# Merge of the DeltaNet inverse in 64x64 quadrants, five unnormalised projections at the start of layer 1, and sums of squares finished on VectorE

## The chip, the cores and the metric

The kernel runs on one core of a Trainium2 chip. The metric is the device time of one execution in microseconds (us), lower is better.

## The reference, cut to what matters

One inference step of a two-layer backbone: 128 context tokens and 256 latent tokens of width 1024, everything in float32. In each layer a modulated RMSNorm feeds one input projection, that feeds three token mixers (windowed attention, multi-head latent attention called MLA below, and a bidirectional gated DeltaNet); a gated sum of the three is projected back and added to the tokens; a second modulated norm and a squared-ReLU MLP follow.

```python
mod = silu(cond) @ w_ada + b_ada                          # shifts, scales and gates of both norms
y = mixer(rmsnorm(x, norm1_g) * (1 + sc1) + sh1)          # w_in, three mixers, w_branch, gates, w_out
x = x + g1 * y
h = rmsnorm(x, norm2_g) * (1 + sc2) + sh2
x = x + g2 * (square(relu(h @ w_ff1)) @ w_ff2)
# DeltaNet, for every chunk of 64 tokens, head and direction:
a_mat = where(strict, (kb @ kc.T) * decay, 0)             # 64 x 64, strictly triangular
t_mat = triangular_solve(eye + a_mat, eye)                # its inverse is wanted
u = t_mat @ (vc * beta);  w = t_mat @ (kb * exp(gc))
```

## The kernel before, in words

All activations lie transposed in SBUF, features on the 128 partitions and the 384 tokens along the row, so a projection is 128x128 weight blocks times 128x384 activations. Each weight tile is split on the chip into a rounded part `whi` (a cast on ScalarE, L147) and the rest `wlo` (a subtraction on VectorE, L148), and a product is three matmuls of 128x384 (`mm3`, L150 to L153: wh·rh, wh·rl, wl·rh; the right side is split in the same way, as `hh` and `hl` for the normed tokens). All other products are plain float32 matmuls through `mm` (L156); one such call shows as two PE instructions in the trace, a bf16 matmul and a transpose as one.

Work is put into three streams with priorities: "chain" (the mixers, whose steps wait for one another), "fill" (projections that are always ready) and "last". A scheduler lays out each engine's order when the kernel is built; on the chip every engine runs its own instructions strictly in that order. So TensorE's fill `mm3` stand between the steps of a chain, in a fixed number. PSUM has eight banks: three "g" (pool `pg`, projections), one "o", two "c" (`bank()`, all small chain products) and a pair "f" (`twin()`).

**Sums of squares and row broadcasts.** `squares` (L207) squares the token tiles on ScalarE and adds them on VectorE (L215), all but the last one, which goes apart. `sums` sums both parts over the partitions with matmuls against a column of ones (six `mm` a call, 128x1). `rsqrt` takes the inverse root on small VectorE operations; `rows` spreads a column over all partitions: `pieces` (L182 to L185) cuts it into three bf16 parts and three bf16 matmuls a row add them. `rstd_rows` is sums, rsqrt and rows in one.

**Start of layer 1 (L461 to L490).** The tokens are the output of layer 0's MLP. While the norm's inverse roots are worked out, two projections (`w_small`, whose output becomes the tile `kab`, and the DeltaNet column 11 of `w_in`) run on tokens that are scaled (`scaled`) but not normalised; then `modulated` (VectorE L227 and L230, ScalarE L229) makes the normalised `hh` and `hl` of all eight token tiles, and the two outputs are multiplied by the inverse roots afterwards (L482 to L487).

**Merge of the inverse (L857 to L899, tiles `Xi`).** Per chunk pair n (3) and direction d (2), four heads at once: M holds the 128x128 matrices. The diagonal 32x32 blocks are inverted on VectorE (L840 to L853, tiles `blk`), transposed as Xc and XcT, and spread into block-diagonal X0 and X0T (L870). Then 32-blocks are joined to 64 and 64 to 128 with five products p1 to p5: p1 and p3 of 128x128, p2 with 64 columns, p4 and p5 of 64x64, each with a PSUM read behind it on VectorE or ScalarE (L878, L886, L888, L895, L897). `M5` (L865) is M times a mask, `M2` (L867) a copy of a corner. GpSimd copies some of M's blocks (L828) and clears the tile of the inverse (L842).

**Modulation.** `ada` multiplies `silu(cond)` by `w_ada` in the fill stream of layer 0's branch merges (`merge(2, more, ...)`, `merge(1, more, ...)`), `ada_sums` does the same for later rounds on VectorE, a step per turn, within ff1 (the MLP's first product) and ff2.

Of the kernel before, what the change touches and what calls it, by code (L numbers as in the profile page):

```python
# [18 lines left out]
P = 128  # L19
DM = 1024  # L20
KT = DM // P
# [23 lines left out]
def trunk(ctx: ExitStack, tc: tile.TileContext, A, O):  # L45
# [57 lines left out]
    mask5 = [cst[:, C_M5 + d * P:C_M5 + (d + 1) * P] for d in range(2)]  # L103
# [3 lines left out]
    bdmask = cst[:, C_BD:C_BD + P]  # L107
# [80 lines left out]
    def rows(b, j0, n):  # L188
# [7 lines left out]
    def sums(ps, col, parts, n):  # L196
        for j in range(n):
            for i, sq in enumerate(parts):
                mm(ps[:, col + j:col + j + 1], sq[:, j * P:(j + 1) * P], ones1, i == 0, i == len(parts) - 1)

    def rstd_rows(parts, scale):

        ps = bank()
        sums(ps, 0, parts, 3)
        return rows(pieces(rsqrt(ps[:, 0:3], 3, scale)), 0, 3)
# [71 lines left out]
    def ada(l, rounds):  # L277

        for r in rounds:
            ps = bank(pg, "g")  # L280
            for k in range(KT):
                for half in range(2):
                    c0 = r * 2048 + half * 1024
                    raw = mk(ada_pool[0], [P, 1024], ada_pool[1], bufs=ada_pool[2])
                    nc.sync.dma_start(raw, A["w_ada"][l, k * P:(k + 1) * P, c0:c0 + 1024])
                    rv = raw.rearrange("p (b g i) -> p g b i", b=8, g=4)
                    for g in range(4):
                        mm(ps[32 * g:32 * g + 32, half * 256:half * 256 + 256].rearrange("p (b i) -> p b i", b=8),
                           cs[:, k, :], rv[:, g], start=k + half == 0, stop=k + half == KT)
                    if k + half == KT:  # L290
                        modulation(l, r, ps)
                    yield

    def ada_sums(l, rounds, pool):


        pick = mk(pool, [P, 2, 32], "pick")
        V.memset(pick, 0.0)
        for s in range(2):
            V.memset(pick[:, s, s:s + 1], 1.0)  # L300
        for r in rounds:
            ps = bank(pg, "g")
            for q in range(4):
                acc = mk(pool, [P, 2, 512], "aacc", bufs=1)
                c0 = r * 2048 + q * 512
                for k in range(KT):
                    raw = mk(pool, [P, 512], "araw", bufs=3)
                    nc.sync.dma_start(raw, A["w_ada"][l, k * P:(k + 1) * P, c0:c0 + 512])
                    for s in range(2):
                        if k == 0:  # L310
                            S.activation(acc[:, s, :], raw, AF.Copy, scale=cs[:, k, s:s + 1])
                        else:
                            V.scalar_tensor_tensor(out=acc[:, s, :], in0=raw, scalar=cs[:, k, s:s + 1], in1=acc[:, s, :],  # L313
                                                   op0=ALU.mult, op1=ALU.add)
                    if k == KT - 1:
                        for s in range(2):
                            av = acc[:, s, :].rearrange("p (b g i) -> p g b i", b=4, g=4)
                            for g in range(4):
                                mm(ps[32 * g:32 * g + 32, q * 128:q * 128 + 128].rearrange("p (b i) -> p b i", b=4),
                                   pick[:, s, :], av[:, g], start=q + s == 0, stop=q + s == 4)  # L320
                        if q == 3:
                            modulation(l, r, ps)
                    yield
# [134 lines left out]
    for l in range(DEPTH):  # L458
# [5 lines left out]
        else:  # L464
# [6 lines left out]
            for w in weights([A["w_small"][l], A["w_in"][l, 11]]):  # L471
                wh, wl = (t.rearrange("p (k c) -> p k c", k=KT) for t in w)
                M = wh.shape[2]
                ps = mk(pg, [P, 512], "g")[:M, :T + 2]
# [4 lines left out]
            for i, ps in enumerate(pss):  # L479
                M = ps.shape[0]  # L480
                t = mk(sp, [48, T], "kab", bufs=1) if i == 0 else mk(sp, [P, T], "sqacc", bufs=1)
                b = mk(sp, [P, 2], "eb")[:M]  # L482
                V.tensor_copy(b, ps[:, T:])
                S.copy(t, ps[:, :T])
                V.tensor_tensor(out=t, in0=t, in1=rb[:M], op=ALU.mult)
                for s, c in STREAMS:
                    S.activation(t[:, c], t[:, c], AF.Identity, bias=b[:, s:s + 1], scale=1.0)  # L487
                early.append(t)
# [50 lines left out]
        kab = early.pop(0)  # L539
        if l == 0:  # L540
            ps, kab = kab, mk(sp, [48, T], "kab", bufs=1)
            S.copy(kab, ps)
        nc.sync.dma_start(O["krT"][l], kab[0:32, 0:128])
        if l == 0:
            nc.sync.dma_start(cst[:, C_M5:], A["const"][:, C_M5:])
            tri = mk(sp, [P, T], "tmp")[:, :2 * P]
# [12 lines left out]
        def g4():  # L559
            return mk(ccp, [P, 4, P], "g", bufs=24)  # L560
# [4 lines left out]
        def h4():  # L565
            return mk(ccp, [P, 4, 64], "h", bufs=3)
# [164 lines left out]
        keys, queries = (mk(ccp, [P, 4, T], "kq", bufs=2) for _ in range(2))  # L731
        done = [conv_silu(ps, 4 + i, keys[:, i, :]) for i, ps in enumerate(early)]
# [56 lines left out]
        for n in range(3):  # L789
# [28 lines left out]
            for d in range(2):  # L818
# [5 lines left out]
                for b in range(4):  # L824
# [31 lines left out]

        Xi = {}  # L857
        half = (slice(0, 64), slice(64, 128))
        for n in range(3):
            for d in range(2):  # L860
                u0 = (2 * n + d) * 4
                hs, os = half[d], half[1 - d]
                M = Mg[n, d]
                M5 = g4()
                V.tensor_tensor(out=M5, in0=M, in1=mask5[d].unsqueeze(1).to_broadcast([P, 4, P]), op=ALU.mult)  # L865
                M2 = h4()
                V.tensor_copy(M2[hs], M[hs, :, os])  # L867
                X0, X0T = M, g4()
                for dst, c in ((X0T, (Xc, XcT)[d]), (X0, (XcT, Xc)[d])):
                    V.tensor_tensor(out=dst.rearrange("p h (b c) -> p h b c", b=4),  # L870
                                    in0=c[:, u0:u0 + 4, :].unsqueeze(2).to_broadcast([P, 4, 4, 32]),
                                    in1=bdmask.rearrange("p (b c) -> p b c", b=4).unsqueeze(1).to_broadcast([P, 4, 4, 32]),
                                    op=ALU.mult)
                ps = bank()
                for h in range(4):
                    mm(ps[:, h * P:(h + 1) * P], M5[:, h, :], X0T[:, h, :])
                WT = g4()
                S.copy(flat(WT), ps)  # L878
                pt = bank()
                for h in range(4):  # L880
                    mm(pt[hs, h * 64:h * 64 + 64], X0[:, h, hs], WT[:, h, hs])
                ps = bank()
                for h in range(4):
                    mm(ps[:, h * P:(h + 1) * P], WT[:, h, :], X0[:, h, :])
                X1T = h4()
                V.tensor_tensor(out=X1T[hs], in0=X0T[hs, :, hs], in1=pt[hs, 0:256].rearrange("p (h c) -> p h c", h=4),  # L886
                                op=ALU.subtract)
                V.tensor_tensor(out=flat(X0), in0=flat(X0), in1=ps, op=ALU.subtract)  # L888
                ps = bank()
                for h in range(4):  # L890
                    mm(ps[os, h * 64:h * 64 + 64], M2[hs, h, :], X1T[hs, h, :])
                W2 = h4()
                S.copy(W2[os].rearrange("p h c -> p (h c)"), ps[os, 0:256])
                ps = bank()
                for h in range(4):  # L895
                    mm(ps[hs, h * 64:h * 64 + 64], W2[os, h, :], X0[os, h, os])
                V.tensor_scalar(out=X0[hs, :, os], in0=ps[hs, 0:256].rearrange("p (h c) -> p h c", h=4), scalar1=-1.0,  # L897
                                scalar2=None, op0=ALU.mult)
                Xi[n, d] = X0  # L899
# [83 lines left out]
        r = pieces(r)  # L983
# [134 lines left out]
        for t in range(NF):  # L1118
# [12 lines left out]
            next(more, None)  # L1131
# [15 lines left out]
    sums(ps, 0, squares(x), 3)  # L1147
# [132 lines left out]
```

## Time and profile before

| what | value |
|---|---|
| median of 3 runs | 1564.96 us (1561.77 to 1565.35) |
| the profiled execution | 1564.52 us |
| its span, first to last instruction | 1562.7 us |
| PE busy | 1521.6 us (97%) |
| DVE, ACT, POOL busy | 1013.9 us (65%), 771.8 us (49%), 12.9 us (1%) |

PE is the matrix engine (TensorE), DVE VectorE, ACT ScalarE, POOL GpSimd. A busy PE is one that has a matmul under way; it says nothing about how much of its array that matmul fills. The 1.8 us between the profiled time and the span lie before the first and after the last instruction.

### The profile page before, as it was taken

What the parts mean: (1) busy time and instruction counts of PE and PEld (TensorE: products, weight loads), DVE (VectorE), ACT (ScalarE), POOL (GpSimd) and SP (SyncE); (2) the same over time, 40 slices, a digit from 0 to 9 for tenths busy, and PEclk for the clock granted to TensorE, in tenths of its full rate; (3) what the DMA queues carried; (4) which work ended last, traced back from release to release, by engine and by line L of the source; (5) the groups of instructions that cost most, each with busy time, mean ns of one, the idle gap of its engine ahead of it and who ended that gap; (6) DMA issues with size and microseconds to landing.
All of it is one profiled execution on the core that took longest, in us unless ns stands there. A gap on an engine that the chain in (4) does not pass through costs nothing.

```text
span 1562.7 us, 25131 instructions
## 1 busy us (share of the span) xinstructions
PE 1521.6 (97%) x9652; PEld 1396.2 (89%) x9652; DVE 1013.9 (65%) x2187; ACT 771.8 (49%) x1522; POOL 12.9 (1%) x34
## 2 busy tenths in 40 slices
PE   5999999999999999999999999999999999999998
PEld 3898788987888999999988987889888999999997
DVE  4667896475435877789986778955655565553332
ACT  3466633346524666643344676334465446664222
POOL 0000100000000000000000001000000000000000
PEclk9999999999999999999998999999999999999999
DMA  9532131143488555578763331311424434433332
GB/s 315 162 103 88 48 95 48 59 145 105 141 291 279 160 175 176 176 236 259 252 187 98 95 95 47 96 49 58 129 61 135 130 118 126 126 122 129 128 122 81
DMA packets 80857, 212.82 MB, mean 136 GB/s; under 512 B 8801, under 2 KB 24545, under 8 KB 80609
## 3 DMA queue, kind: packets, MB, share of 16 engines
q1 hardware_dynamic: 80736, 211.21, 42.7%
q8 instruction: 76, 1.25, 0.3%
q14 instruction: 45, 0.36, 0.1%
HBM read 204.59 MB, written 4.75 MB: 134 GB/s over the span
## 4 chain that ended last, share of the span: by engine, by line
PE 86%; DVE 8%; DMA 4%; ACT 1%; issue 1%; SPq 0%; DVEq 0%; ACTq 0%
PE g L151 22%; PE g L153 22%; PE g L152 22%; PE c L156 9%; PE f L156 3%; DMA araw<-in_w_ada_dram 2%; PE o L156 2%; PE f L443 2%; DVE wlo L148 2%; PE g L156 1%; DVE h L847 1%; DVE blk L849 1%; DMA mraw<-in_w_ada_dram 1%; PE c L151 1%; PE c L153 1%
## 5 line engine op out<-in xcount | busy, mean ns | idle before, releaser
L147 ACT CAST whi<-raw 128x1024 fp32r<-128x1024 f32 x268 | 280.8, 1048 | 463.6 <-PE g L152 408.0
L153 PE MATMUL g<-hh,wlo 128*128 128x384 f32 (+1 forms) x1440 | 495.2, 345 | 2.8 <-DVE wlo L148 2.7
L151 PE MATMUL g<-hh,whi 128*128 128x384 f32 (+1 forms) x1440 | 494.8, 345 | 3.1 <-ACT hh L229 1.5
L152 PE MATMUL g<-hl,whi 128*128 128x384 f32 (+1 forms) x1440 | 493.6, 344 | 1.3 <-DVE hl L230 1.0
L148 DVE TENSOR_TENSOR wlo<-raw,whi 128x1024 fp32r<-128x1024 f32 x268 | 326.0, 1217 | 168.5 <-PE g L153 123.1
L151 PEld LDWEIGHTS g<-hh,whi 128*128 128x128 f32 x1440 | 272.2, 189 | 14.9 <-issue 6.3
L153 PEld LDWEIGHTS g<-hh,wlo 128*128 128x128 f32 x1440 | 272.5, 189 | 12.4 <-DVE wlo L148 6.0
L152 PEld LDWEIGHTS g<-hl,whi 128*128 128x128 f32 x1440 | 272.2, 189 | 8.1 <-issue 2.7
L151 PE MATMUL g<-fh,whi 128*128 128x384 f32 x512 | 172.9, 338 | 0.0
L152 PE MATMUL g<-fl,whi 128*128 128x384 f32 x512 | 172.1, 336 | 0.0
L153 PE MATMUL g<-fh,wlo 128*128 128x384 f32 x512 | 172.1, 336 | 0.0
L313 DVE SCALAR_TENSOR_TENSOR aacc<-araw,cs,aacc 128x512 f32<-128x512 f32 x168 | 116.5, 747 | 11.0 <-DMA araw<-in_w_ada_dram 6.9
L151 PEld LDWEIGHTS g<-fh,whi 128*128 128x128 f32 x512 | 96.2, 188 | 1.6 <-issue 1.6
L152 PEld LDWEIGHTS g<-fl,whi 128*128 128x128 f32 x512 | 96.3, 188 | 0.0
L153 PEld LDWEIGHTS g<-fh,wlo 128*128 128x128 f32 x512 | 96.3, 188 | 0.0
L156 PE MATMUL c<-g,g 128*128 128x128 f32 (+1 forms) x608 | 77.5, 274 | 3.6 <-DVE g L870 3.1
L156 PEld LDWEIGHTS c<-g,g 128*128 128x128 f32 (+1 forms) x608 | 69.9, 182 | 11.3 <-ACT g L878 4.0
L151 PE MATMUL g<-brh,whi 128*128 128x384 f32 x192 | 66.4, 346 | 0.4 <-ACT whi L147 0.4
L152 PE MATMUL g<-brl,whi 128*128 128x384 f32 x192 | 65.7, 342 | 0.0
L153 PE MATMUL g<-brh,wlo 128*128 128x384 f32 x192 | 65.6, 342 | 0.0
L424 ACT ACTIVATE at_p<-at_p,at_nm 128x384 f32<-128x384 f32 (+1 forms) x96 | 51.8, 541 | 24.7 <-DVE at_nm L421 23.9
L148 DVE TENSOR_TENSOR fl<-fa,fh 128x384 fp32r<-128x384 f32 x64 | 35.6, 556 | 41.9 <-ACT fh L147 41.9
(312 smaller groups left out, 1862.3 us busy)
## 6 DMA issues: line engine op xcount, KB each, us to landing
raw<-in_w_ff_dram SPq DMA_DIRECT2D x128, 512.0 KB, 3.6
raw<-in_w_in_dram SPq DMA_DIRECT2D x102, 512.0 KB, 3.6
araw<-in_w_ada_dram SPq DMA_DIRECT2D x96, 256.0 KB, 3.4
raw<-in_w_branch_dram SPq DMA_DIRECT2D x24, 512.0 KB, 3.6
araw<-in_w_ada_dram SPq DMA_DIRECT2D x24, 512.0 KB, 6.4
raw<-in_w_out_dram SPq DMA_DIRECT2D x16, 512.0 KB, 4.3
mraw<-in_w_ada_dram SPq DMA_DIRECT2D x8, 512.0 KB, 9.2
mraw<-in_w_ada_dram SPq DMA_DIRECT2D x16, 256.0 KB, 7.6
```

The costliest lines, as they stand in the source:

```text
L147: S.copy(hi, src)
L148: V.tensor_tensor(out=lo, in0=src, in1=hi.bitcast(F32), op=ALU.subtract)
L151: PE.matmul(ps, lhsT=wh, rhs=rh, start=start, stop=False)
L152: PE.matmul(ps, lhsT=wh, rhs=rl, start=False, stop=False)
L153: PE.matmul(ps, lhsT=wl, rhs=rh, start=False, stop=stop)
L156: return PE.matmul(ps, lhsT=lhsT, rhs=rhs, start=start, stop=stop)
L313: V.scalar_tensor_tensor(out=acc[:, s, :], in0=raw, scalar=cs[:, k, s:s + 1], in1=acc[:, s, :], op0=ALU.mult, op1=ALU.add)
L424: S.activation(sm[:, :nk], sm[:, :nk], AF.Exp, bias=nm[:, u:u + 1], scale=-1.0, accum_out=den[:, u:u + 1])
L443: PE.transpose(pt[:, j * P:(j + 1) * P], ps_[half, n][:, c * P:(c + 1) * P], ident)
L847: V.tensor_tensor(out=tmp, in0=Cb[:, j + 1:, j:j + 1].to_broadcast([P, r, w]), in1=X[:, j:j + 1, :w].to_broadcast([P, r, w]), op=ALU.mult)
L849: V.tensor_tensor(out=X[:, j + 1:, :w], in0=X[:, j + 1:, :w], in1=tmp, op=ALU.subtract)
```

## The change: what it does

1. `sums` and `squares`: all squares are added on VectorE, one addition more a call; summing over partitions takes three matmuls instead of six. There are nine calls: four a layer and the final norm.
2. `rows`: one float32 transpose of the broadcast column a row, instead of three bf16 matmuls, and no `pieces` there (48 rows in ten calls).
3. `ada`: a step does both halves of a k (eight matmuls, seven of them issued after the first), and the merges take steps at other rates. `ada_sums` has its blocks in another order, and ff1 takes 40 of its steps instead of 32. `araw` has four buffers instead of three.
4. Layer 1 begins with five unnormalised projections (`w_small` and columns 11 to 14) in the three "g" banks and the twin; their outputs stay in PSUM and are normalised later in the chain stream (`normalised`), from an SBUF copy `rbs` of the inverse roots.
5. The merge takes the three chunk pairs in seven runs. All products are 64x64 quadrants (64 rows of contraction, 64 outputs, 64 columns), upper and lower row halves alternating, the two halves into different banks. X0 and X0T are half as wide; the diagonal 32-blocks of M are cleared by 48 GpSimd memsets instead of multiplied by a mask (`M5` and `M2` are gone). `tc.issue_after` keeps the matmuls of a run behind its first ones.
6. Buffers: 22 `g` instead of 24, seven `h` instead of three, own tiles for keys and queries.

```diff
-            for i in range(3):
-                mm(ps[:, j * P:(j + 1) * P], b[i][:, j0 + j:j0 + j + 1].to_broadcast([P, P]), ident16, i == 0, i == 2)
+            PE.transpose(ps[:, j * P:(j + 1) * P], y[:, j0 + j:j0 + j + 1].to_broadcast([P, P]), ident)
...
+    def sums(ps, sq):
+        for j in range(3):
+            mm(ps[:, j:j + 1], sq[:, j * P:(j + 1) * P], ones1)
...
-            if i < len(tiles) - 2:
-                V.tensor_tensor(out=acc, in0=acc, in1=sq, op=ALU.add)
-        return acc, sq
+            V.tensor_tensor(out=acc, in0=acc, in1=sq, op=ALU.add)
+        return acc
...
-            for w in weights([A["w_small"][l], A["w_in"][l, 11]]):
+            banks = [mk(pg, [P, 512], "g") for _ in range(3)] + twin()
+            for ps, w in zip(banks, weights([A["w_small"][l]] + [A["w_in"][l, 11 + i] for i in range(4)])):
...
             hh, hl = modulated(rb, gp1, mod0, 0)
...
+            rbs = mk(sp, [P, T], "sqacc", bufs=1)
+            S.copy(rbs, rb)
+            early += pss
...
+        def normalised(t, ps):
+
+            M = ps.shape[0]
+            b = mk(sp, [P, 2], "eb")[:M]
+            V.tensor_copy(b, ps[:, T:])
+            V.tensor_tensor(out=t, in0=ps[:, :T], in1=rbs[:M], op=ALU.mult)
+            for s, c in STREAMS:
+                S.activation(t[:, c], t[:, c], AF.Identity, bias=b[:, s:s + 1], scale=1.0)
+            return t
...
+            for d in range(2):
+                for b in range(4):
+                    G.memset(Mg[n, d][32 * b:32 * b + 32, :, 32 * b:32 * b + 32], 0.0)
...
+        def p1(n, ps):
+            return each([(d, b) for d in range(2) for b in range(2)],
+                        lambda i, h: (i[1], lambda: mm(ps[i[1]][half[i[1]], at(i[0], h)], Mg[n, i[0]][half[i[1]], h, half[i[1]]],
+                                                       X0T[n, i[0]][half[i[1]], h, :])))
...
+        spread(0)
+        spread(1)
+        t1, t2 = twin(), pair()
+        run(p1(0, t1), p1(1, t2))
+        e1(0, t1)
+        e1(1, t2)
+        t1, t2 = twin(), pair()
+        run(p3(0, t2), p2((0, 1), t1))
+        e2(0, t1)
+        e2(1, t1)
+        e3(0, t2)
+        spread(2)
+        t1, t2 = twin(), pair()
+        run(p3(1, t2), p4((0, 1), t1))
...
-        merge(2, more, (1, 1))
+        merge(2, more, (1, 0))
...
-            ada_pool[:] = pool, "araw", 3
-            merge(1, more, (3, 3))
+            ada_pool[:] = pool, "araw", 4
+            merge(1, more, (1, 2))
...
-            next(more, None)
+            for _ in range(2 if t % 4 == 3 else 1):
+                next(more, None)
```

How instructions now stand, engine by engine. On PE at the start of layer 1, the kernel before goes from the second projection (into `g_8404`), with the pieces of the inverse roots among it, to the first projections on normalised tokens (`g_8626` and `g_8665`, rows apart), with the product of `kab` between them:

```order
L151 MATMUL g_8404<-hh_8303,whi_8400 128x386
...
L156 LDWEIGHTS piece_1555_8283
L156 MATMUL c_8291<-ident_3_85,piece_1555_8283 128x128
...
L152 MATMUL g_8404<-hl_8328,whi_8400 128x386
...
L151 MATMUL g_8626<-hh_8430,whi_8622 128x384
...
L151 MATMUL g_8665<-hh_8430,whi_8661 128x384
...
L156 MATMUL c_8536<-cst_83,kab_8501 128x48
...
L152 MATMUL g_8665<-hl_8440,whi_8661 128x384
```

After the change, the same place on PE has five projections (`g_8300` to `f_8303` and a second half of the twin) with the three sums and the three transposes inside the first two of them:

```order
L150 MATMUL g_8300<-hh_8236,whi_8306 48x386
...
L155 MATMUL c_8214<-cst_83,sqacc_8191 128x1 x3
...
L150 MATMUL g_8301<-hh_8236,whi_8336 128x386
...
L191 MATMUL c_8230<-cst_83,rs_y_8219 128x128 x3
...
L150 MATMUL g_8302<-hh_8236,whi_8366 128x386
...
L150 MATMUL f_8303<-hh_8236,whi_8396 128x386
...
L150 MATMUL g_8693<-hh_8455,whi_8689 128x384
...
L155 MATMUL c_8555<-cst_83,kab_8541 128x48
```

So three projections of 24 matmuls each moved ahead of the first one that needs normalised tokens; the first of these (`g_8693`) takes the bank that `kab` leaves.

On PE in the merge of layer 0, before, one visit of the chain (chunk pair 0, direction 0) reads, with six fill matmuls ahead of the next visit:

```order
L156 MATMUL c_2724<-g_2721,g_2717 128x128 x4
...
L153 MATMUL g_2145<-hh_348,wlo_2142 128x384
...
L156 MATMUL c_2731<-g_2729,g_2434 64x64 x4
L156 MATMUL c_2736<-g_2434,g_2729 128x128 x4
L156 MATMUL c_2744<-h_2741,h_2719 64x64 x4
L151 MATMUL g_2145<-hh_462,whi_2141 128x384
...
L156 MATMUL c_2751<-g_2434,h_2749 64x64 x4
L156 MATMUL c_2764<-g_2761,g_2757 128x128 x4
```

After the change, the end of run 2 (p2 of chunk pairs 0 and 1 into the twin `f_2784`), the two fill matmuls behind it and the beginning of run 3 (p3 of chunk pair 1, into new "c" banks) read on PE:

```order
L155 MATMUL f_2784<-h_2781,queries_2728 64x64
L155 MATMUL f_2784<-h_2778,queries_2728 64x64
L150 MATMUL g_2157<-brh_1959,whi_2106 128x384
L151 MATMUL g_2157<-brl_1960,whi_2106 128x384
L155 MATMUL c_2837<-queries_2728,h_2778 64x64
L152 MATMUL g_2157<-brh_1959,wlo_2107 128x384
```

The banks `c_2837` and `c_2836` are those that run 2 wrote as `c_2786` and `c_2785`; on DVE the reads that empty them stand around those of the twin:

```order
L962 TENSOR_TENSOR g_2420<-blk_2727,c_2786 64x4x64
L962 TENSOR_TENSOR g_2420<-blk_2727,c_2785 64x4x64
L962 TENSOR_TENSOR g_2429<-blk_2727,c_2785 64x4x64
L957 TENSOR_TENSOR h_2819<-blk_2727,f_2784 64x256
L957 TENSOR_TENSOR h_2821<-blk_2727,f_2784 64x256
L957 TENSOR_TENSOR h_2823<-queries_2728,f_2784 64x256
L957 TENSOR_TENSOR h_2825<-queries_2728,f_2784 64x256
L962 TENSOR_TENSOR g_2429<-blk_2727,c_2786 64x4x64
```

So where PE before waited for one read of one group, run 3 now stands behind eight reads.

On POOL, before, the clearing of the tile of the inverse follows the last copy; afterwards (second fence, the third chunk pair) two groups of memsets stand between:

```order
L828 COPY blk_2385<-g_2590 32x4x32 x4
L842 MEMSET blk_2617 128x1024
L843 MEMSET blk_2617 128x32
```

```order
L847 COPY blk_2371<-g_2592 32x4x32 x4
L852 MEMSET g_2592 32x4x32 x4
L852 MEMSET g_2601 32x4x32 x4
L864 MEMSET blk_2627 128x1024
L865 MEMSET blk_2627 128x32
```

## Rows read from the trace of the kernel before

**Rows 1.** The page: span, and busy time by engine.

```profile
span 1562.7 us, 25131 instructions
PE 1521.6 (97%) x9652; PEld 1396.2 (89%) x9652; DVE 1013.9 (65%) x2187; ACT 771.8 (49%) x1522; POOL 12.9 (1%) x34
```

**Rows 2.** Windows by stage: length, busy PE, PEld, DVE, ACT, POOL; PEclk, DMA, GB/s.

```profile
228.00:265.00 37.00, 36.41 (x303) 30.86 (x304) 29.38 (x46) 9.64 (x17) 0.00 (x0) 1.00 0.14 44
430.00:500.00 70.00, 68.40 (x507) 59.11 (x506) 30.89 (x50) 21.94 (x31) 0.00 (x0) 1.00 0.87 290
530.00:668.00 138.00, 138.00 (x838) 135.71 (x839) 104.21 (x187) 92.62 (x168) 0.00 (x0) 1.00 0.55 170
815.63:833.47 17.84, 14.27 (x49) 11.04 (x49) 15.33 (x47) 9.83 (x24) 0.00 (x0) 0.71 0.30 93
1006.90:1043.60 36.70, 36.60 (x304) 31.04 (x305) 29.21 (x45) 9.64 (x17) 0.00 (x0) 1.00 0.15 44
```

**Rows 3.** Groups of PE instructions by form, merge of layer 0 (228.2 to 265 us).

```profile
L156 PE MATMUL c<-g,g 128*128 128x128 f32 x97 | 14.1, 287 | 1.6 <-DVE g L870 1.6
L156 PE MATMUL c<-h,h 64*64 64x64 f32 x48 | 4.0, 224 | 0.0
```

**Rows 4.** Chain of waits within that merge: start, length, piece.

```profile
246.68 0.60 PE c L156 x8
247.28 0.37 PE g L151
247.65 0.89 PE c L156 x8
248.54 0.18 PE g L152
```

**Rows 5.** Timeline of PE: attention scores in row halves, MLA scores, and the merge's first products.

```profile
80.49 0.92 PE L156 MATMUL f<-kA,qA 64*128 64x384 f32 x4
...
352.94 1.45 PE L156 MATMUL f<-kp,qp 96*128 96x384 f32 x4
...
228.24 1.16 PE L156 MATMUL c<-g,g 128*128 128x128 f32 x8 [1.57 <-DVE g L870]
```

**Rows 6.** Groups of DVE instructions by form, merge of layer 0 (228 to 265 us).

```profile
L870 DVE TENSOR_TENSOR g<-blk,cst 128x512 f32<-128x512 f32 x12 | 12.4, 1047 | 0.2
L148 DVE TENSOR_TENSOR wlo<-raw,whi 128x1024 fp32r<-128x1024 f32 x3 | 3.7, 1221 | 0.5 <-PE g L153 0.5
L897 DVE TENSOR_SCALAR g<-c 64x256 f32<-64x256 f32 x6 | 2.5, 421 | 1.5 <-PE c L156 1.4
```

**Rows 7.** Timeline of DVE at the start of layer 1.

```profile
813.30 1.00 DVE L227 SCALAR_TENSOR_TENSOR tmp<-x,gp,c 128x128 f32<-128x128 f32 x3 [0.79 <-PE c L156]
...
822.99 1.15 DVE L230 SCALAR_TENSOR_TENSOR hl<-tmp,mod,hh 128x256 fp32r<-128x256 f32 x3
824.06 0.54 DVE L485 TENSOR_TENSOR kab<-kab,c 48x384 f32<-48x384 f32 x1
```

**Rows 8.** Groups of PE instructions in 815.63 to 833.47 us: the one not of a projection.

```profile
L576 PE MATMUL c<-cst,kab 48*128 48x48 f32 x3 | 0.8, 327 | 1.1 <-ACT kab L487 1.1
```

**Rows 9.** Chain of waits at a norm's sums and rows, and three transposes.

```profile
529.97 1.23 PE c L156 x12
...
534.84 0.18 PE c L156
...
535.43 0.54 PE c L156 x8
...
193.38 0.33 PE f L443 x3
```

**Rows 10.** Timeline of POOL and DVE ahead of layer 0's inversion of the 32-blocks.

```profile
180.33 1.79 POOL L828 COPY blk<-g 32x128 f32<-32x128 f32 x4 [6.75 <-DVE g L821]
182.18 0.96 POOL L842 MEMSET blk<- 128x1024 f32 x1
...
185.85 0.19 DVE L847 TENSOR_TENSOR h<-blk,blk 128x31 f32<-128x31 f32 x1
```

More of the change, by code (lines that the diff above doesn't have):

```diff
@@ L726, in advance @@
                     next(fill, None)
[L731 to L732 removed]
+        keys, queries = (mk(ccp, [P, 4, T], name, bufs=1) for name in ("keys", "queries"))
+        done = [conv_silu(ps if l == 0 else normalised(flat(g4())[:, :T], ps), 4 + i, keys[:, i, :]) for i, ps in enumerate(early)]
         n_done = len(done)
@@ new lines, in trunk, with pair, run @@
+        X0T = {(n, d): x0s[n % 2][:, 2 + d] for n in range(3) for d in range(2)}
+        WT, X1T, W2 = {}, {}, {}
+        at = lambda q, h: slice(q * 256 + h * 64, q * 256 + h * 64 + 64)
+        side = lambda q: slice(q * 256, q * 256 + 256)
+        def pair():
+            return [bank(), bank()]
+        def run(*sets):
+            firsts, rest = [], []
+            for makes in sets:
+                lo = [m for r, m in makes if r == 0]
+                hi = [m for r, m in makes if r == 1]
+                order = [m for two in zip(hi, lo) for m in two]
+                firsts += order[:2]
+                rest += order[2:]
+            with ExitStack() as after:
+                for m in firsts:
+                    after.enter_context(tc.issue_after(m().ins))
+                for m in rest:
+                    m()
@@ L860, in trunk, with p5, spread @@
+        def p5(ns, pt):
+            return each([(n, d) for n in ns for d in range(2)],
+                        lambda i, h: (1 - i[1], lambda: mm(pt[1 - i[1]][half[i[1]], at(i[0] % 2, h)], W2[i][half[1 - i[1]], h, :],
+                                                           Mg[i][half[1 - i[1]], h, half[1 - i[1]]])))
+        def spread(n):
             for d in range(2):
                 u0 = (2 * n + d) * 4
-                hs, os = half[d], half[1 - d]
-                M = Mg[n, d]
-                M5 = g4()
@@ L886, in trunk @@
[L886 to L893, printed above, removed]
@@ new lines, in e1, with e2, e3 @@
+        def e1(n, ps):
+            for d in range(2):
+                WT[n, d] = h4()
+                for b, hs in enumerate(half):
+                    (S.copy if b else V.tensor_copy)(flat2(WT[n, d][hs]), ps[b][hs, side(d)])
+        def e2(n, pt):
+            for d in range(2):
+                X1T[n, d] = h4()
+                V.tensor_tensor(out=X1T[n, d][half[d]], in0=X0T[n, d][half[d]], in1=heads(pt[d][half[d], side(n % 2)]), op=ALU.subtract)
+        def e3(n, ps):
+            for d in range(2):
+                for b, hs in enumerate(half):
+                    V.tensor_tensor(out=Mg[n, d][hs, :, hs], in0=X0[n, d][hs], in1=heads(ps[b][hs, side(d)]), op=ALU.subtract)
@@ new lines, in e4, with e5 @@
+        def e4(n, pt):
+            for d in range(2):
+                W2[n, d] = h4()
+                S.copy(flat2(W2[n, d][half[1 - d]]), pt[d][half[1 - d], side(n % 2)])
+        def e5(n, pt):
+            for d in range(2):
+                V.tensor_scalar(out=Mg[n, d][half[d], :, half[1 - d]], in0=heads(pt[1 - d][half[d], side(n % 2)]), scalar1=-1.0,
+                                scalar2=None, op0=ALU.mult)
+                Xi[n, d] = Mg[n, d]
+        spread(0)
+        spread(1)
+        t1, t2 = twin(), pair()
@@ L903, in new_values @@
+        run(p3(2, t2), p2((2,), t1))
+        e2(2, t1)
+        e3(2, t2)
+        t1 = twin()
+        run(p4((2,), t1))
+        e4(2, t1)
+        t1 = twin()
+        run(p5((2,), t1))
+        e5(2, t1)
         def new_values(n, d, r):
```

132 lines of the change are left out of this document (68 added, 64 removed).

## The prediction, made before the change was timed

> **What bounds the kernel now.** I read the page first: PE is busy for 1521.6 of 1562.7 us [rows 1], so what the change does off PE counts only where PE waits. Then the windows by stage: in most of them PE is busy throughout at a granted clock of 1.00, the upper of its two levels, and one stretch stands out, 815.63 to 833.47 us at the start of layer 1, where the clock is 0.71 and PE's 17.84 us hold only 49 instructions [rows 2]. Then the groups and the chain within the merge: TensorE is "busy" there too, but with 241 small products (97, and three forms of 48) among 62 fill matmuls (303 in all), so the question is how fast these run [rows 2 to 4]. The sum is made against the profiled execution, 1564.5 us, which is 0.4 us off the median of 1564.96; the 1.8 us outside the span I leave as they are.
>
> **Merge, price before.** The stage from 228.24 us (the first product [rows 5]) to 265.00 us is 36.8 us. A fill matmul costs 0.175 us (0.18 and 0.17 in turn [rows 4]); 62 of them are 10.9, which leaves **25.9 us** a layer for the merge's own products. Layer 1 has a stage of the same length [rows 2]. The parts agree: eight instructions of 128 columns take 0.89, eight of 64 columns 0.60, and the fill matmul behind the latter 0.37 instead of 0.18 [rows 4].
>
> **Merge, price after.** Now 168 calls, 336 instructions, all 64 columns wide. By columns: 0.89/8 is 0.111 for 128, so 0.056 for 64, in all 18.7 us one after the other. Upper and lower row halves alternate, and whether they overlap is the main unknown. The nearest row: four instructions of 384 columns on 64-row halves (`kA,qA`) take 0.92, four of 384 columns on 96 rows (`kp,qp`) 1.45 [rows 5]. I take this ratio, 0.63: 11.8 us. Entering costs 0.60 − 8×0.056 = 0.15 and leaving 0.2 [rows 4], with about 10 visits of the chain, as fill still stands between the runs: 3.5. Sum 15.3, that is 10.6 less than 25.9.
>
> The runs bring new waits, since each needs what VectorE (DVE) makes of the one before. A spread half as wide is half of 1.05, so 0.52; a read of 64x256 is 0.42 [rows 6]. By the order shown: the first run needs spreads for two chunk pairs, eight instead of two. Its first products wait for two half ones (about 1.3 instead of 1.57 [rows 5]), its last for all: five more are 2.6 us, of which 1.4 is covered by what PE issues in between, so 1.2. Run 3 takes "c" banks that are empty only after eight reads: 3.4 us, less 0.6 for the products of run 2 that end behind the first reads and 0.3 for two fill matmuls, so 2.5. Run 5 follows run 4 with no fill, 0.5; run 7 waits for a copy by ScalarE, 0.4. Together 5.9, or 4.3 more than the 1.57 of before. So 10.6 − 4.3 = 6.3 a layer, **−12.6 us** for two. Bounds: with no overlap 25.9 − 18.7 − 3.5 − 4.3 = −0.6 (nothing gained); with full overlap and no new wait 25.9 − 9.4 − 3.5 = 13.0 a layer.
>
> **Start of layer 1.** In the 17.84 us PE did 46 matmuls of a projection and three for `kab` [rows 2, 8]: at 0.175 and 0.11 (three transposes of 128 columns take 0.33 [rows 9]) that is 8.4, so 9.4 are lost, to waits for normalised tokens and to matmuls at the lower clock. `modulated` holds DVE from 813.30 to 824.06, and the multiplication of `kab` comes behind it [rows 7]. Now three more projections, 72 matmuls or 12.6 us, stand in front of the first that needs normalised tokens: PE reaches that one at about 815.6 + 12.6 − 0.7 (fewer sums and pieces ahead) = 827.5. DVE starts `modulated` about as before and has two more `wlo` (1.22 each [rows 6]) in its way, so it is through at 824.6 + 2.4 − 1 (the pieces that are gone) = 826, with `kab` ready behind it. PE then has no gap to wait in and no reason to fall to the lower clock. I take **−8.9**, 0.5 short of all; bounds −3 (three of the five banks come free late) and −9.4. What is late next: the three further outputs wait in PSUM for `normalised`, while the next projections need their "g" banks; their multiplications come directly behind `kab`'s on DVE (0.54 each [rows 7]), within one projection's 4.2 us.
>
> **Sums.** A call's six products are 12 instructions in 1.23 us [rows 9]; half of them are gone, 0.62. It counts in seven of the nine calls (the first norm waits for its data, and at the final norm the added addition is on the path): **−4.3**, bounds 3.5 and 4.3. In the others that addition falls under fill.
>
> **Rows.** Nine bf16 matmuls take 0.18 + 0.54 = 0.72; three transposes 0.33 [rows 9]. That is 0.4 in six calls (not the first, and the one at layer 1's start is counted there): 2.3. An output norm has 36 at 0.54/8 = 0.068, 2.4 us, against 12 at 0.11, 1.3: 1.1, twice 2.2. **−4.5**, bounds 2 and 4.5.
>
> **POOL.** Four 32x128 copies take 1.79, and the clearing (0.96) ended near 183.3, when DVE needed it at 185.85: a slack of 2.5 us [rows 10]. Eight memsets now stand ahead of it. The trace has no such memset; between almost nothing and a copy's 0.45 each, 0 to 3.6 us. DVE loses the masking M5 of the same place, but the inversion is then up to 1.1 late, and fill's `wlo` behind it on DVE. **+1.2** for two layers, bounds 0 and 2.4.
>
> **The rest at nothing.** The modulation steps move by eight into ff1, where DVE is busy 104.2 of 138.0 us [rows 2]; if that cover were gone, eight steps would cost some 10 us. In 430 to 500 us, where DMA is at 0.87 and PE short by 1.6 [rows 2], a fourth `araw` may give back up to 1.5. Buffer counts order nothing that PE waits for.
>
> Sum: −12.6 − 8.9 − 4.3 − 4.5 + 1.2 = −29.1, from 1564.5 to **1535.5 us**.
>
> **Rivals.** A: the quadrants do not overlap. For it: 64 columns are so short that issuing may set the pace; against it: the halves of rows 5. The merge then gives nothing (+1.2), and the time is 1549.
>
> B: the start of layer 1 stays a gap, because five banks are held and `kab`'s is freed behind all of `modulated`. For it: that order on DVE; against it: 12.6 us of cover. With 3 instead of 8.9: 1541.5.
>
> C, on the other side: the matmuls kept behind the first of each run hold PE's whole queue, fill too, until DVE is done. DVE's work in a layer's merge is 12 spreads (6.2), 30 reads (12.6) and three `wlo` (3.7) [rows 6], 22.5. If none of it were covered, the stage would be 15.3 + 10.9 + 22.5 = 48.7 instead of 36.8 + 1.6, a loss of 10.3 a layer; with −16.5 from the other parts 1564.5 + 20.6 − 16.5 = 1569. It is slower once the uncovered part passes about 20.4 us a layer, 2.9 a run; my waits come to 5.9 in all. Against it: fill stands between most runs. The Trainium skill states it as a rule ("TensorEngine Tiling (Array Packing)", Performance Considerations, PSUM Bottleneck): tiling speeds TensorE up but not the emptying of PSUM, which may then become the limit. By that rule, taken to its end, the time is that of C; the trace of before shows DVE busy 29.4 of the merge's 37 us [rows 2], near but not at it.
>
> D: full overlap and no new wait: 26.0 instead of 12.6, so 1522. The same page (Overview, Theoretical Speedup) gives up to 2× for a dimension of at most 64. The rows of the halves show 1/0.63, 1.6×.
>
> **How the numbers follow.** Chances: forecast 0.48, A 0.17, B 0.13, D 0.14, C 0.06, and 0.02 that nothing moves. Differences within 0.3% (4.7 us) cannot be told from none here. Forecast, A, B and D are all faster, 0.92; C is slower, with a share of what lies between, 0.05; the same 0.03. The terms' own bounds around the forecast give some 1528 to 1543; the range takes in D and A to their middle: 1521 to 1550.
>
> **What would show it.** In the new trace: merge products of 64x64 with starts of two halves a few ns apart, and a merge stage of about 30 us instead of 37; a wait of PE for DVE L962 ahead of run 3; no lower clock between 815 and 835 us, with the first matmul on `hh` from `modulated` straight behind the fifth projection; six instructions instead of twelve for a sum, in about 0.6 us; `h<-blk,blk` on DVE up to a microsecond behind its transpose. Wrong would be: pairs one after the other, PE idle before more than two runs a layer by over 2 us, or a gap left at the start of layer 1.

## The result, and the profile after

| | median | span of the profiled run | PE busy |
|---|---|---|---|
| before, 4 runs | 1563.53 us | 1562.7 us | 1521.6 us |
| after, 4 runs | 1538.70 us (1537.98 to 1539.57) | 1537.8 us | 1488.8 us |

The ratio is 0.9841 (95% interval 0.9824 to 0.9858): 24.8 us faster. The forecast was 1535.5, range 1521 to 1550. The total came out; its two largest terms did not, as the views show. Span and busy time from the page, after:

```profile
span 1537.8 us, 25236 instructions
PE 1488.8 (97%) x9694; PEld 1369.7 (89%) x9694; DVE 995.1 (65%) x2163; ACT 769.8 (50%) x1527; POOL 22.4 (1%) x82
```

PE lost 32.8 us of busy time but the span only 24.9: some 8 us of the saving became waiting. Windows of the run after, to be held against [rows 2] (columns as there):

```profile
430.00:500.00 70.00, 70.00 (x490) 63.92 (x489) 41.42 (x69) 25.04 (x36) 0.00 (x0) 1.00 0.83 280
...
813.16:821.30 8.14, 0.00 (x0) 0.01 (x1) 8.14 (x23) 5.51 (x13) 0.00 (x0) 0.80 0.46 133
821.30:830.00 8.70, 8.68 (x31) 7.86 (x32) 6.34 (x29) 4.89 (x13) 0.00 (x0) 0.60 0.02 4
```

The first row is the modulation stage: PE no longer falls short there (68.40 of 70.00 before). The other two are the start of layer 1: there still is a gap, now in one piece. The timeline of PE after shows its two ends, and DVE's what happens in it:

```profile
812.82 0.34 PE L152 MATMUL f<-hh,wlo 128*128 128x386 f32 x1
821.32 0.66 PE L150 MATMUL g<-hh,whi 128*128 128x384 f32 x1 [8.16 <-DVE kab L551]
...
823.65 0.52 PE L150 MATMUL g<-hh,whi 128*128 128x384 f32 x1
```

```profile
804.79 1.22 DVE L147 TENSOR_TENSOR wlo<-raw,whi 128x1024 fp32r<-128x1024 f32 x1 [2.94 <-issue]
809.02 1.22 DVE L147 TENSOR_TENSOR wlo<-raw,whi 128x1024 fp32r<-128x1024 f32 x1 [3.01 <-PE f L152]
810.17 1.15 DVE L226 SCALAR_TENSOR_TENSOR hl<-tmp,mod,hh 128x128 fp32r<-128x128 f32 x3
...
819.57 1.15 DVE L226 SCALAR_TENSOR_TENSOR hl<-tmp,mod,hh 128x256 fp32r<-128x256 f32 x3
820.63 0.54 DVE L551 TENSOR_TENSOR kab<-g,sqacc 48x384 f32<-48x384 f32 x1
```

The added projections run without a break up to 812.82, but DVE stands idle twice for 3 us beside them and writes the first normalised `hl` at 810.17, when the fifth projection has begun. From there it works through eight tiles, kab's normalisation comes last, and PE waits 8.16 us. The granted clock is 0.60 of full speed in the 8.7 us behind the gap. At this place, the gaps and what projection matmuls take beyond their usual 0.1756 us (from start to start) add up in the two traces to 9.8 us lost before (3.6 + 6.2) and **11.8 after** (8.2 + 3.6).

In the merge it is the other way round. PE and, below it, DVE in the merge of layer 0, after:

```profile
226.34 0.33 PE L155 MATMUL f<-blk,g 64*64 64x64 f32 x4 [1.67 <-DVE blk L944]
...
235.52 0.32 PE L155 MATMUL c<-queries,h 64*64 64x64 f32 x2
237.89 0.27 PE L155 MATMUL c<-queries,h 64*64 64x64 f32 x1
...
241.50 0.30 PE L155 MATMUL c<-blk,g 64*64 64x64 f32 x2 [0.76 <-DVE g L962]
```

```profile
234.16 1.20 DVE L962 TENSOR_TENSOR g<-blk,c 64x256 f32<-64x256 f32 x3 [0.83 <-PE c L155]
...
236.97 0.42 DVE L962 TENSOR_TENSOR g<-blk,c 64x256 f32<-64x256 f32 x1
```

Run 3 begins at 235.52, right behind the third read (ended 235.36), without a gap: one of its two banks has had both of its reads by then. So it does not stand behind all eight. Its product in the other follows at 237.89, 0.5 us behind the eighth read, and 11 fill matmuls stand between. So the wait of 2.5 us that I had put here does not exist. The products in detail, run 2 of the same merge:

```profile
234.53 0.22 PE L155 MATMUL f<-h,queries 64*64 64x64 f32 x1
234.54 0.22 PE L155 MATMUL f<-h,blk 64*64 64x64 f32 x1
234.59 0.22 PE L155 MATMUL f<-h,queries 64*64 64x64 f32 x1
```

Two instructions of opposite row halves start within 0.01 us of each other, and the next pair 0.06 later. Added up from start to start, the merge products took 44.9 us for 480 instructions before (0.0935 each) and 24.9 us for 672 after (0.0371 each); the gaps ahead of them went from 3.6 to 5.5 us in all. The stages of the two layers, from the first of these products to the last, as windows of the run after:

```profile
226.34:251.85 25.51, 24.68 (x394) 21.11 (x394) 20.66 (x43) 8.77 (x19) 0.00 (x0) 0.93 0.15 44
992.82:1019.70 26.88, 25.13 (x401) 21.10 (x401) 20.54 (x43) 8.65 (x20) 0.00 (x0) 1.00 0.20 61
```

In layer 1 the clock is at its upper level throughout, and the 336 products take 11.9 us (0.0354 each); in layer 0 it is lower at the start, and they take 13.0.

Of the smaller parts, a sum is six instructions in 0.73 us, and on POOL the eight memsets take 1.96 us:

```profile
514.26 0.73 PE L155 MATMUL c<-cst,sqacc 128*128 128x1 f32 x6
```

```profile
181.61 1.96 POOL L852 MEMSET g<- 32x128 f32 x8
183.62 0.96 POOL L864 MEMSET blk<- 128x1024 f32 x1
...
185.20 0.20 DVE L869 TENSOR_TENSOR h<-blk,blk 128x31 f32<-128x31 f32 x1
```

The clearing ends at 184.8 and DVE comes to it at 185.20 after other work: no delay.

### The profile page after: what moved, and what is told of

It reads as the page before. It is cut to its first block, busy times and chain, and to the rows that moved or that the text cites. A ratio compares the mean times of both kernels' runs of the same rounds, so it can differ in the third digit from the quotient of the medians.

```text
span 1537.8 us, 25236 instructions
## 1 busy us (share of the span) xinstructions
PE 1488.8 (97%) x9694; PEld 1369.7 (89%) x9694; DVE 995.1 (65%) x2163; ACT 769.8 (50%) x1527; POOL 22.4 (1%) x82
## 5 line engine op out<-in xcount | busy, mean ns | idle before, releaser
L150 PE MATMUL g<-hh,whi 128*128 128x384 f32 (+1 forms) x1424 | 489.0, 345 | 8.9 <-DVE kab L551 8.2
L152 PE MATMUL g<-hh,wlo 128*128 128x384 f32 (+1 forms) x1424 | 488.4, 344 | 4.0 <-DVE wlo L147 3.9
L151 PE MATMUL g<-hl,whi 128*128 128x384 f32 (+1 forms) x1424 | 486.2, 342 | 0.0
L150 PEld LDWEIGHTS g<-hh,whi 128*128 128x128 f32 x1424 | 268.8, 189 | 20.5 <-issue 16.6
L152 PEld LDWEIGHTS g<-hh,wlo 128*128 128x128 f32 x1424 | 268.6, 189 | 13.0 <-DVE wlo L147 8.2
L151 PEld LDWEIGHTS g<-hl,whi 128*128 128x128 f32 x1424 | 268.7, 189 | 5.9 <-issue 2.6
L347 DVE SCALAR_TENSOR_TENSOR x<-g,mod,x 128x128 f32<-128x128 f32 x64 | 23.7, 412 | 51.0 <-PE g L152 47.6
L1231 ACT ACTIVATE fa<-fa,fb 128x128 f32<-128x128 f32 (+1 forms) x128 | 51.1, 446 | 0.7 <-DVE fa L1229 0.7
```

Of the source, the lines that this page charges most:

```text
L150: PE.matmul(ps, lhsT=wh, rhs=rh, start=start, stop=False)
L151: PE.matmul(ps, lhsT=wh, rhs=rl, start=False, stop=False)
L152: PE.matmul(ps, lhsT=wl, rhs=rh, start=False, stop=stop)
L347: V.scalar_tensor_tensor(out=x[k][:, c], in0=ps[:, c], scalar=m[:, b0 + k, s:s + 1], in1=x[k][:, c], op0=ALU.mult, op1=ALU.add)
L1231: S.activation(a[:, c], a[:, c], AF.Relu, bias=b[:, s:s + 1])
```

## The experiments

The theory after this profile: at the start of layer 1 the scaled tokens of the five projections and the normalised ones share the same eight pairs of tiles (`hidden()`, tags `hh` and `hl`, eight buffers), so `modulated` cannot write a tile before the fifth projection has read it; more projections ahead only put this off. Rivals were DVE's queue (a `wlo` ahead of `modulated` that waits for one of two buffers), the bank that kab holds, and DVE's work in the whole stretch. For the merge: that alternating row halves overlap. All ratios are to the kernel before on the same chip; the changed kernel has 0.9841.

**Own tiles** for the scaled tokens:

```diff
-            hi, lo = hidden()
+            hi, lo = hidden() if pool is None else (mk(pool, [P, T + 2], f"x{s}{k}", F32R) for s in ("h", "l"))
...
-            xh, xl = scaled(gp1, mod0, 0)
+            xe = ExitStack()
+            xh, xl = scaled(gp1, mod0, 0, area(xe, "own", "right"))
...
+            xe.close()
             hh, hl = modulated(rb, gp1, mod0, 0)
```

> The changed kernel, with tiles of their own for the scaled tokens at the start of layer 1 (xh, xl), instead of the eight pairs that the normalised tokens (hh, hl) are then written into. Theory 1, shared tiles: modulated could not write hh of a token tile before the fifth projection had read it, so the three added projections gave no cover. Then modulated runs beside the projections, PE's gap of 8.2 us and the lower clock behind it (3.3 us) are gone, all but some 2 us: about 1538.7 - 9.5 = 1529 us. Rival, VectorE's queue: modulated stood behind two wlo subtractions that waited for one of two wlo tiles; those are as before, so a gap of some 5 to 8 us stays: 1536 to 1539 us.

Measured: 1534.01 us, ratio 0.9800 (0.9785 to 0.9814). The gap of 8.16 us is gone, with the two `wlo` tiles as they were, which speaks against DVE's queue. But the time lies between theory and rival: about 6 us came of it, or 4 against the changed kernel's second measurement (below). A new wait stands at the other end, with the clock lower behind it, as PE's timeline and a window of this run show:

```profile
790.65 1.20 PE L150 MATMUL g<-xh,whi 128*48 128x386 f32 x3 [2.15 <-ACT xh L146]
```

```profile
790.00:801.00 11.00, 10.03 (x44) 8.23 (x45) 8.19 (x37) 6.50 (x25) 0.00 (x0) 0.69 0.22 67
```

The new tiles lie where tiles of the MLP lay, which its last matmul still reads, so scaling starts late.

**Two projections**, normalised at once, in the changed kernel (the loop and lines of before in place of the new ones):

```diff
-            banks = [mk(pg, [P, 512], "g") for _ in range(3)] + twin()
-            for ps, w in zip(banks, weights([A["w_small"][l]] + [A["w_in"][l, 11 + i] for i in range(4)])):
+            for w in weights([A["w_small"][l], A["w_in"][l, 11]]):
...
```

> The changed kernel, but layer 1 begins with two unnormalised projections, normalised at once, as before. By the traces the start loses 11.8 us with five and lost 9.8 with two (gaps, and matmuls at the lower clock): 1538.7 - 2 = 1536.7 us. By the prediction's step five are worth 8.9: 1547.6 us.

Measured: 1536.94 us, 0.9811 (0.9792 to 0.9830). Five projections are worth nothing over two, or cost a little; the gain of 8.9 us that the prediction gave this step is ruled out.

**Old merge** in the changed kernel:

```diff
-        spread(0)
-        spread(1)
-        t1, t2 = twin(), pair()
-        run(p1(0, t1), p1(1, t2))
...
+                M5 = g4()
+                V.tensor_tensor(out=M5, in0=M, in1=mask5[d].unsqueeze(1).to_broadcast([P, 4, P]), op=ALU.mult)
...
```

> The changed kernel, with the merge as before (five products per chunk pair and direction, 128 wide, mask, no memsets, 24 g and three h tiles). Theory: the quadrants are worth what the trace's starts of PE instructions say, 43.9 us before against 24.9 after in both layers, less 1.9 of added waits, plus 1 of the fill behind a visit: about 18 us, so 1557 us. Rival, the prediction's size: 12.6, so 1551 us.

Measured: 1561.13 us, 0.9972 (0.9961 to 0.9983). The merge, with its memsets and buffers, is worth 0.0131, 20.5 us, and so more than four fifths of the whole change. That is 2.5 us more than I expected. From start to start over the whole traces of this run and of the changed kernel, the projection matmuls differ by 4.5 us (in part the slower fill behind the old visits, for which I had put 1), all other products by 19.2, and PE's waits by 1.8 the other way.

**Not alternating**:

```diff
-                order = [m for two in zip(hi, lo) for m in two]
+                order = hi + lo
```

> The changed kernel, with the same quadrant products, but in each group of a run all of one row half first and then all of the other. Theory: two row halves overlap only when they follow each other; then an instruction goes from 0.037 to about 0.056 us, 672 of them, 12.6 us, some of which hides the waits for VectorE: 1546 to 1551 us. Rival: the short products are as fast one behind the other in the same half: 1538 to 1540 us.

Measured: 1549.65 us (1543.40 to 1552.50), 0.9894 (0.9869 to 0.9920), 8.3 us slower than the changed kernel. From start to start the 672 instructions take 39.4 us instead of 24.9, 0.0586 us instead of 0.0371 on average. But not all of that is order, as the windows of the two merges in this run show, to be held against those above:

```profile
225.94:264.82 38.88, 38.84 (x405) 35.26 (x405) 20.68 (x43) 10.20 (x25) 0.00 (x0) 0.74 0.15 42
1002.31:1031.87 29.56, 29.50 (x403) 26.68 (x403) 20.66 (x43) 10.16 (x25) 0.00 (x0) 1.00 0.19 55
```

In layer 0 PE ran at the lower clock level for some 21 of the 38.9 us, in layer 1 at the upper one throughout. In layer 1 the 336 products take 17.0 us (0.0507 each) instead of 11.9 (0.0354). So the order is worth 5.1 us a layer in the products at the same clock, and the alternation does make the halves overlap; the gaps ahead of the products shrink from 5.5 to 3.0 us in both layers, so part of the loss covers waits, and part of the 8.3 us is the clock of layer 0. (The edit also changes which two products of a group the others are kept behind.)

**Kab first**: the normalisation of kab ahead of `modulated`, and with it the copy `rbs` that it reads:

```diff
+            kab = normalised(mk(sp, [48, T], "kab", bufs=1), pss.pop(0))
             hh, hl = modulated(rb, gp1, mod0, 0)
```

> The changed kernel, with the normalisation of kab put ahead of modulated, so that the first g bank comes free early; the scaled and the normalised tokens still share their tiles. Theory 1, shared tiles: PE no longer waits for the bank, but follows modulated tile by tile from the fifth projection's end, at 1.31 us a tile instead of 0.53: the single gap of 8.2 us becomes eight small ones, its first projection on normalised tokens ends with modulated, some 6 us earlier than now, and the lower clock stays: 1532 to 1535 us where the changed kernel has 1538.7. Rival, the bank alone (rival B of the prediction): all of the gap is gone, 1528 to 1530 us.

Measured: 1538.57 us (1533.01 to 1543.37), 0.9840 (0.9813 to 0.9867): slower than both expectations, its interval is wide, and no gain is shown. The profiled execution is the fastest of the four (1533.01). In its trace PE follows `modulated` in small steps, as in the kernel before:

```profile
813.12 0.44 PE L150 MATMUL g<-hh,whi 128*128 128x384 f32 x1 [0.57 <-ACT hh L225]
813.88 0.45 PE L151 MATMUL g<-hl,whi 128*128 128x384 f32 x1 [0.33 <-DVE hl L226]
...
817.33 0.69 PE L151 MATMUL g<-hl,whi 128*128 128x384 f32 x1 [1.14 <-DVE hl L226]
```

So the bank alone is not the cause: had it been, PE would not wait for `modulated` here.

**The changed kernel again**, on the chip of this and the next run:

> The changed kernel itself once more, as a reference on the same chip: 1538 to 1541 us.

Measured: 1536.38 us, 0.9827 (0.9813 to 0.9842). That is below what I expected, and the two measurements of one kernel lie 2 us apart; below that nothing is read from a ratio here.

**Half own**: kab first, own tiles for the scaled tokens 4 to 7 only, and `modulated` in the order 4 to 7, 0 to 3:

```diff
+            hi, lo = hidden() if pool is None or k < 4 else (mk(pool, [P, T + 2], f"x{s}{k}", F32R) for s in ("h", "l"))
...
+            hh, hl = modulated(rb, gp1, mod0, 0, [4, 5, 6, 7, 0, 1, 2, 3])
```

> Kab first, and tiles of their own for the scaled tokens 4 to 7 only; modulated makes tiles 4 to 7 first and 0 to 3 behind the fifth projection. The run with tiles of its own for all eight lost 2.2 us ahead of the first projection, since these tiles took the place of MLP tiles that are read to the end; tiles 0 to 3 are now written before that, as in the changed kernel. Theory 1: neither that gap nor the one of 8.2 us, and no lower clock at the start of layer 1: about 1538.7 - 11 = 1528 us. If the gaps only move: 1532 to 1535 us, like the run with own tiles.

Measured: 1538.61 us, 0.9837 (0.9820 to 0.9853): a miss. Both gaps are gone, PE runs to 823 us with one wait of 0.25, and then it waits three times for the chain that hangs on `modulated`, and its clock falls. Timeline of PE and windows of this run:

```profile
824.64 0.41 PE L150 MATMUL g<-hh,whi 128*128 128x384 f32 x1 [0.73 <-ACT g L480]
825.68 0.90 PE L689 MATMUL f<-cst,tmp 128*128 128x128 f32 x3 [0.45 <-DVE g L653]
...
828.49 0.80 PE L155 MATMUL c<-cst,g 128*128 128x1 f32 x3 [1.26 <-ACT g L764]
```

```profile
825.00:828.00 3.00, 1.77 (x7) 1.04 (x5) 3.00 (x7) 2.71 (x8) 0.00 (x0) 0.60 0.08 22
828.00:832.00 4.00, 3.52 (x15) 3.52 (x16) 3.90 (x9) 1.85 (x6) 0.00 (x0) 0.50 0.38 131
832.00:839.00 7.00, 7.00 (x25) 7.00 (x25) 0.00 (x0) 0.45 (x1) 0.00 (x0) 0.50 0.27 75
839.00:850.00 11.00, 11.00 (x65) 9.81 (x63) 8.47 (x34) 3.96 (x9) 0.00 (x0) 0.99 0.35 97
```

The waits are 2.4 us; the lower level, from 825 to 839 us, costs more than they do. Either DVE's work in the whole stretch was now the limit, or only what it can begin behind the fifth projection, four tiles and the chain after them. Four kernels asked which.

**Half less** leaves out the low parts of four token tiles:

```diff
+                if len(los) < n_lo:
+                    V.scalar_tensor_tensor(out=lo[:, c], in0=t[:, c], scalar=sh[:, sh0 + k, s:s + 1],
...
```

> Half own, but at the start of layer 1 modulated leaves out the low parts (L226) of four of the eight token tiles; the tiles of the other four stand in for them. That takes 3.3 us of VectorE's work out of the stretch and nothing from PE. Theory, VectorE's work sets this stretch: it is busy 9.8 of 10, 5.9 of 6 and 11 of 11 us there in the run before, so 3.3 us less lets PE's waits between 824 and 830 us (2.7) and the lower clock behind them (6.8) go, wholly or in part: 1530 to 1535 us, where half own had 1538.6. Rival: the waits have another cause; 1537 to 1540 us.

Measured: 1525.30 us, 0.9742 (0.9728 to 0.9757), 13 us less than half own by the medians and 15 by the ratios, more than expected. The left-out work lies in the tail behind the fifth projection (tiles 0 to 3), so it fits both readings. The waits and the lower clock went away together.

**Half pool** and **own pool** take three `wlo` off DVE, which lie ahead of that tail:

```diff
-            split(raw[:, :n], hi[:, :n], lo[:, :n])
+            split(raw[:, :n], hi[:, :n], lo[:, :n], G if j in on_pool else V)
```

> Half own, with the wlo subtractions of three of the five projections on GpSimd instead of VectorE; the same arithmetic. Theory, VectorE's work: 3.4 us less on it, 1530 to 1535 us, if GpSimd does 128x1024 within the 4.2 us of a projection. Rival: GpSimd is slower than that, or slows VectorE, and PE waits for wlo in place of it: 1539 us or more.

> Own tiles, with the same three subtractions on GpSimd. Theory: in that run PE waited little behind the start, so there is less to win, 1531 to 1534 us. Rival, as for half pool: PE waits for wlo, 1536 us or more.

Measured: half pool 1538.65 us, 0.9828 (0.9813 to 0.9842), as half own; own pool 1542.03 us, 0.9856 (0.9838 to 0.9874), slower than own tiles. POOL's timeline in half pool:

```profile
798.27 4.85 POOL L147 TENSOR_TENSOR wlo<-raw,whi 128x1024 fp32r<-128x1024 f32 x2 [613.86 <-PE g L152]
805.14 2.41 POOL L147 TENSOR_TENSOR wlo<-raw,whi 128x1024 fp32r<-128x1024 f32 x1 [2.02 <-PE g L152]
```

A subtraction is 2.4 us there, within the 4.2 us of a projection, and PE has the same three waits at 825.05, 826.08 and 828.53. So taking 3.4 us of DVE's work away ahead of the tail changes nothing. In own pool PE waits 3.00 us for kab, not for a `wlo` as the rival had it, which is one reason that it lost.

**Two shared**: as half own, but only tiles 0 and 1 share theirs (`k < 2`, order 2 to 7, 0, 1). Nothing is left out.

> Half own, but only tokens tiles 0 and 1 share their tiles; 2 to 7 have their own, and modulated makes these first. Nothing is left out. Theory, shared tiles: what VectorE can begin only behind the fifth projection's reads sets PE's waits after it; this tail shrinks from four tiles (5.2 us) to two (2.6), nearly as much as in the run that left out four low parts (3.3 us, 1525.3 us): 1524 to 1531 us. Rival, VectorE's work in the whole stretch: it is the same as in half own, so 1536 to 1540 us.

Measured: 1528.54 us (5 runs), 0.9777 (0.9761 to 0.9794): with the tail at two tiles two waits of 0.15 us or more are left between 812 and 840 us, 1.10 (shown) and 0.33 for ACT's `g` of L764, and the clock stays at its upper level. PE's timeline and a window of this run:

```profile
813.35 0.44 PE L152 MATMUL g<-hh,wlo 128*128 128x384 f32 x1 [1.10 <-DVE wlo L147]
```

```profile
812.00:840.00 28.00, 26.57 (x162) 24.23 (x161) 25.30 (x91) 16.67 (x40) 0.00 (x0) 1.00 0.46 142
```

It does all of the computation and is 10 us faster than the changed kernel by its ratio (0.9777 against 0.9841, or 7.8 against the second measurement): the fastest of the complete kernels here.

The executions already differ by up to 5 us where none of these edits acts (the last MLP matmul of layer 0 begins at 786.5 to 791.7 us). So here is the stretch alone, in each profiled execution, from the start of that matmul to the first merge product of layer 1:

| kernel | stretch |
|---|---|
| changed, its two measurements | 202.1 and 201.5 us |
| two projections | 201.0 us |
| own tiles; own pool | 199.3; 205.5 us |
| kab first | 199.7 us |
| half own; half pool | 202.6; 203.0 us |
| half less | 190.8 us |
| two shared | 192.9 us |

By this measure own tiles and kab first gain only some 2 us, two shared gains 9, and half less is 12 ahead of half own.

**Old sums**, six matmuls and one addition less:

```diff
+            for i, sq in enumerate(parts):
+                mm(ps[:, j:j + 1], sq[:, j * P:(j + 1) * P], ones1, i == 0, i == len(parts) - 1)
```

> The changed kernel with six matmuls a sum as before, and one addition less on VectorE. By the starts of PE instructions in the two traces the 54 instructions are worth 6.7 us in nine calls: 1543 to 1546 us. Rival, the prediction: seven calls count, 4.3 us, 1541 to 1543 us.

Measured: 1537.97 us, 0.9821 (0.9807 to 0.9836): by the ratio not slower than the changed kernel in either of its measurements, and outside both expectations. The 54 instructions are back in the trace with 6.6 us, but no such time shows. PE's waits are 39.0 us in all there, against 42.1 and 40.9 in the changed kernel, which covers a part. The run says nothing below some 2 us, and speaks against a gain of 4.3.

## Why the prediction was right in sum, and where it failed

**Merge: −12.6 foretold, about −20.5 measured.** The mechanism held; a term of the sum was mis-sized. The products themselves are 24.9/2 = 12.4 us a layer, foretold 11.8, and 22.4 plus the slower fill behind each visit before, foretold 25.9 together. Wrong were the new waits: 4.3 us a layer foretold, (5.5 − 3.6)/2 = 1.0 in the trace. The step that failed reads "Run 3 takes "c" banks that are empty only after eight reads", 2.5 us a layer: one bank was free after three, and 11 fill matmuls covered the rest. I had read the order of DVE's reads but not which of them frees which bank.

**Overlap.** I priced a pair by 0.92 against 1.45 [rows 5], 0.63. At the upper clock level, in layer 1, alternating is 0.0354 against 0.0507 not alternating, 0.70. That the averages of both layers, 0.0371 and 0.0586, give 0.63 too is chance, since layer 0 of the second ran at the lower level for more than half of its merge. A running pair of opposite halves takes 0.058 us, as long as one instruction alone, and entering and leaving a run cost the rest. The Trainium skill ("TensorEngine Tiling (Array Packing)", Overview, Theoretical Speedup) gives up to 2× for a dimension of at most 64. By that rule, the trace agrees within a run; over all products of layer 1 the order gives 1.4×. Rival A is ruled out by this run, and C by the gaps, 5.5 us in both layers together. The Trainium skill ("TensorEngine Tiling (Array Packing)", Performance Considerations, PSUM Bottleneck) warns that emptying PSUM may become the limit, which did not come true here: DVE was busy 20.7 of the 25.5 us of layer 0's merge. For the merge alone, rival D came closer than the forecast.

**Start of layer 1: −8.9 foretold, 0 to +5 measured.** One of the prediction's own signs of being wrong, "a gap left at the start of layer 1", came true. The failed step is "DVE starts `modulated` about as before", and from it "PE then has no gap to wait in". I had taken 12.6 us of added projections as cover. They are none, since `modulated` writes into the tiles that they read: before it could begin as the second projection ran, now as the fifth did. Rival B had the outcome and gave kab's bank as the cause; kab first shows that the bank was the last of the waits and not the first. That the shared tiles set the time rests on four kernels: own tiles (the gap goes), half own and two shared (the fewer tiles share, the less PE waits behind the fifth projection), and half pool (less of DVE's work as a whole changes nothing). What they leave open is the order: each edit of the tiles also lets the scheduler lay out DVE's queue anew, and no run holds that order fixed.

**Sums and rows: −4.3 and −4.5 foretold.** Old sums shows no gain that can be measured; which part of the step failed (the count of seven calls, or cover by PE's waits) stays open. The rows were not undone by themselves; from start to start, 144 bf16 products took 8.6 us before and 48 transposes 5.2 after, so 3.3 us of PE. Whether all of it is time is open.

**POOL: +1.2 foretold, nothing seen.** Eight memsets are 1.96 us, below the slack of 2.5 that I had read; a memset is 0.245 us, little more than half of a copy's 0.45, which I had taken as the bound.

**The rest.** The fourth `araw` (or the new rates) gave back 1.6 us of PE's waits, at my bound of 1.5; which of the two did was not tried.

So the terms are roughly −20.5, +2, 0, at most −3.3, 0 and −1.6 instead of −12.6, −8.9, −4.3, −4.5, +1.2 and 0. That the sum came out is luck: a merge 8 us better than foretold and a start of layer 1 some 11 us worse cancel, and the sum alone would have taught nothing.

## What to carry to other kernels

Work put ahead of a wait covers it only if what is waited for can begin earlier than that work ends. Before counting added work as cover, look up which buffers the awaited writes go into and who reads them last; here eight shared tile pairs made the cover worthless, and freeing six of them was worth 8 to 10 us. Small products of 64 rows gain from the order in which they are issued, upper and lower half in turn, about as much as from their size: at the upper clock 22.4 us a layer became 17.0 by the quadrants and 11.9 by the order.

## What the hardware showed that I had not expected

In half own, waits of 0.73, 0.45 and 1.26 us within 4 us went with 14 us at the lower clock level (0.50, 1.2 GHz), and a wait of 1.10 us in two shared with none. Half less, without the first three, was 12 to 15 us faster for 3.3 us of work left out. The wait ahead of layer 0's merge is another case: 1.57 us before, with no fall of the clock, 1.67 in the changed kernel, with the lower level until 231 us, and 1.68 without alternation, with the lower level from 227 to nearly 248 us. What decides it is not settled by these runs. But a comparison of two kernels has to look at the granted clock of each stage first: between half own and half less the clock moved more time than the waits did.
